# Dense weights and the experts' gate and up matrices stored in HBM in the blocks in which they are loaded

## The chip, the core and the metric

The kernel runs on one core of a Trainium2 chip. The metric is the device time of one execution in microseconds. Before the change it is 3160.01 us, the median of three runs (3159.78 to 3161.74).

The engines are named as in the profile: PE is TensorE (matmul; PEld its weight loads), DVE is VectorE, ACT is ScalarE, POOL is GpSimd and SP is SyncE, which here only issues loads. HBM is the memory outside the core; SBUF is the memory on it, with 128 partitions. An array is fetched from HBM into SBUF by a DMA, which 16 transfer engines carry out in packets; a packet is one contiguous run of bytes.

## The reference

Three layers work on 256 tokens of width 2048, all in float32. What matters here is which weights they read.

```python
u = x @ w_in                                # [256, 2048] @ [2048, 10544]
y_r = _rwkv7_mixer(u_r, ...)                # a recurrence over the tokens, 16 heads
y_m = _mlstm_mixer(u_m, ...)                # a gated linear attention, 8 heads
mix = (sigmoid(g_r) * (y_r @ w_br) + sigmoid(g_m) * (y_m @ w_bm)) @ w_out
x = _layer_norm(ALPHA * x + mix)
moe = _hier_moe(x, ...)                     # 32 experts, two per token:
#       (silu(xb @ w_gate[e]) * (xb @ w_up[e])) @ w_down[e]
ple = sigmoid(x @ w_pg) * (p @ w_ple)
x = _layer_norm(ALPHA * x + moe + ple)
# second block, even layer: rmsnorm, x @ w_in_even [2048, 6144],
#   banded attention and a state-space scan (S5) with w_glu, then @ w_out_even
# second block, odd layer: rmsnorm, x @ w_in_odd [2048, 8208],
#   causal attention with a forget gate, 16 heads of 128, then @ w_out_odd
```

An expert's `w_gate` and `w_up` are [2048, 512] and its `w_down` is [512, 2048], 4 MiB each.

## The kernel before

**Dense products.** The class `Stream` holds a list of pieces. A piece is a block of a weight matrix of 512 KB and the products that use it. `cols` (line 124) takes 4 row blocks of 128 rows by 256 columns and computes the transposed output, 24 matmuls of 256 columns a piece; `rows` (line 158) takes 2 row blocks by 512 columns, 12 matmuls of 512 columns a piece. Each weight is split into a high part and a low part: `split` (line 265) copies the raw piece `wraw` into `whi` on ScalarE (line 266) and subtracts on VectorE to get `wlo` (line 267; on GpSimd in a few places). Each product is then made three times (lines 147, 149, 151, or 173 to 175): high by high, high by low, low by high.

`step` (line 83) emits the products of one piece at a time. Before that it splits up to two pieces ahead and issues the fetches of two or three raw buffers more. `weave` (line 111) puts such steps between the steps of the dependent chains (recurrence, attention, S5, routing), so that the dense products fill TensorE while a chain waits. The fetch of a piece is one DMA on SP's queue:

```python
def load(self, src):                                              # line 121
    return lambda raw: self.nc.sync.dma_start(raw, src.rearrange("(k p) n -> p k n", p=128))
```

The source is a slice of the matrix as the reference has it, row by row. A partition of the destination gets one row out of each row block: in `cols` 4 runs of 256 floats (1 KB each), in `rows` 2 runs of 512 floats (2 KB each). The runs of neighbouring partitions lie one matrix row apart: 10544 floats in `w_in`, 6144 in `w_in_even`, 8208 in `w_in_odd`, 2048 in `w_out` and most others.

At the start `lora` (line 386) has a piece of 96 columns that are gathered from three places in `w_in`: for each of its four fetches VectorE clears a part of the raw buffer and SP issues three narrow loads (32, 8 and 8 columns).

**Experts.** `expert_order` (line 1219) lists the loads of all 32 experts in the order of use: gate and up by turns in four steps of 512 rows each, then down in four steps of 128 rows, 1 MiB each. `load_expert` (line 1244) takes the next one into a ring of ten buffers `ew` of [128, 2048] and issues it on SP; the first ten go on ScalarE's queue during the out projection, and two more go into a spare tile. A partition gets 4 runs of 2 KB of gate or up, or one run of 8 KB of down. Experts go in pairs: gather of the tokens (line 1273), gate and up (line 1320), the activation on ScalarE and VectorE (lines 1328 and 1329), transposes (line 1332), down (line 1376), and the weighted sum back to the tokens (line 1304). The products with `w_pg` and `w_ple` are woven into the first pairs.

`overflow` (line 1170) is a loop over the experts for tokens past 64 an expert; it runs only when there are any.

**Odd layer.** `odd` (line 1851) queues a 16-column piece, and then for each of eight groups of 256 columns the pieces of k, q and z (4 each, by `cols`), with 8 pieces of v (by `rows`) ahead of every second group, and weaves the attention of 16 heads among them, three steps of the stream to one of the chain. SP's queue also carries two small loads `nk<-cum` for each head.

**What sets the order.** The order in which each engine runs its instructions is written by a planner when the kernel is built (`schedule_with_timeline_sim=True`, line 2194), which has its own estimates of times; `issue_after` pins some instructions behind others. The arrays are laid out on the host before the launch (`prep`, line 2129).

Of the kernel before, what the change touches and what calls it, by code (L numbers as in the profile page):

```python
# [16 lines left out]
D = 2048  # L17
S = 256
KT = D // 128
KCH = 4  # L20
# [16 lines left out]
# column offsets of w_in  # L37
# [4 lines left out]
class Piece:  # L42
    """a block of a weight matrix and the products that use it, in steps"""
# [5 lines left out]
class Stream:  # L49
    """dense products, emitted step by step; the weights are fetched and split ahead of their use"""  # L50
    AHEAD = 2

    def __init__(self, K):
        self.K, self.nc = K, K.nc
        self.pieces, self.nf, self.ns, self.nm, self.sub = [], 0, 0, 0, 0
        # instructions of ScalarE and GpSimd that the splits come after, with the low parts on GpSimd
        self.after = None
# [25 lines left out]
    def step(self):  # L83
        """one step of products (about 1.3 us of TensorE); False when none is left"""
# [38 lines left out]

    def cols(self, w, r0, kts, c0, ncols, xh, xl, evac, cw=256, fetch=None):
        """out^T[cols, tok] = (x @ w[:, c0:c0+ncols])^T; evac(tile of 128 columns, psum [m, 256])"""
        nc, K = self.nc, self.K
        for c in range(0, ncols, cw):
# [3 lines left out]
            for k0 in range(0, kts, KCH):  # L131
# [3 lines left out]
                else:  # L135
                    f = self.load(w[r0 + k0 * 128:r0 + (k0 + kn) * 128, c0 + c:c0 + c + n])
# [46 lines left out]
    def tokens_first(self, n):  # L183
        """the last n pieces, of rows(): token tile 0 of all of them before token tile 1"""
# [11 lines left out]
class Sums:  # L196
    """2^(1/4) x1 and what is added to it [128, 2, D], in a tile that is taken at the first sum"""
# [4 lines left out]
    def __call__(self, i, q, src):  # L202
        """src added to columns 512 q .. of token tile i"""
# [12 lines left out]
class Ker:  # L216
# [60 lines left out]
    def recip1p(self, t):  # L277
        """1 / (1 + t) in place"""
# [4 lines left out]
    def shift(self, out, ps, mu, omu):  # L283
        """out [m, 256] from psum [m, 256]"""
# [4 lines left out]
    # ================= RWKV-7 =================  # L289
    def rwkv_consts(self, pool):  # L290
# [18 lines left out]
        # blocks of 16: minus row j of its block on each partition; the block's mask; unit rows; halves of 32  # L309
# [71 lines left out]
    def sig(self, t):  # L381
        """sigmoid in place"""
# [3 lines left out]
    def lora(self, pool, xh, xl, ig, fg):  # L386
        """zw | za | zg and the mLSTM's gate logits"""
# [13 lines left out]
        self.st.cols(A["w_in"], 0, KT, C_L, 256, xh, xl, evac)  # L401
# [20 lines left out]
        self.st.cols(None, 0, KT, 0, 96, xh, xl, evac2, fetch=fetch)  # L422
# [7 lines left out]
    def rwkv_proj(self, q, W, C, xh, xl):  # L430
        """k, r, v of heads 4q .. 4q + 3: two tiles of 128 channels each"""
        cx = {}
        for nm, mu, c, pool in (("k", "mu_k", C_K, W), ("r", "mu_r", C_R, W), ("v", "mu_v", C_V, C)):
# [8 lines left out]
            self.st.cols(self.A["w_in"], 0, KT, c + 256 * q, 256, xh, xl, evac)  # L442
# [28 lines left out]
    def rwkv_prep(self, q, W, C, cx):  # L471
        """the factors of the chunked form, before the chains"""
# [16 lines left out]
        # decay and in-context rate  # L489
# [15 lines left out]
        # L = cumsum of sigmoid in each chunk; the log decay is -KAPPA * L  # L505
# [21 lines left out]
        # kk = k * k_k, normalised over each head  # L527
# [24 lines left out]
        # k' = k * (1 + (a - 1) k_a)  # L552
# [13 lines left out]
        # bonus  # L566
# [14 lines left out]
    def rwkv_post(self, q, C, cx, y):  # L581
        """head norm (v was centred, so d is: its mean square is the variance), bonus, gate"""
# [52 lines left out]
    def rwkv_pair(self, i, W2, cx):  # L635
        """two heads: the delta rule in four chunks of 64 tokens"""
# [1561 lines left out]
```

## Time and profile before

| | before |
|---|---|
| median of 3 runs | 3160.01 us (3159.78 to 3161.74) |
| span of the profiled execution | 3162.0 us; of the time around it the page shows nothing |
| TensorE matmul busy | 2922.4 us, 92% |
| VectorE, ScalarE, GpSimd busy | 49%, 33%, 16% |
| read from HBM | 727.00 MB, 235 GB/s over the span |
| packets | 441588; 229904 of them under 2 KB, 424592 under 8 KB |
| dense loads of 512 KB | 560 (`w_in` 164, `w_in_odd` 128, `w_in_even` 96, four matrices with 32, two with 16, `w_glu` 8, `w_ple` 4) |
| expert loads of 1 MiB | 384 |

The page's slices show the stages: the first layer's mixers from 0 to about 950 us, the experts to about 2050, the even layer to about 2530, the odd layer to about 3115, then the final norm. Busy time of TensorE is modelled to the end of each matmul's pipeline, so consecutive matmuls overlap in it, and a matmul at the lower of the two clocks (1.2 instead of 2.4 GHz) is busy longer. "PEclk" is the mean granted share of the full clock in a stretch. The DMA share is the mean busy share of the 16 transfer engines; in a full queue it comes out a little above 1.

### The profile page before, as it was taken

The page shows a single profiled execution, that of the slowest core. Times are in us where ns is not written, and L with a number is a line of the kernel's source. Part 1 is how long each engine was busy: PE and PEld are TensorE (multiplying, and loading weights), DVE is VectorE, ACT ScalarE, POOL GpSimd, SP SyncE. Part 2 cuts the span into 40 slices and gives each one's busy share as a digit, 9 for nine tenths or more (in the row PEclk, how much of TensorE's full clock was granted, in tenths as well). Part 3 has the DMA queues.
Part 4 walks back from the last instruction along what each step waited for, and adds up shares of the span by engine and source line. Part 5 has one row for each costly group of instructions (what it writes and reads, how often), then busy time and mean ns, then how long its engine had stood idle before and what let it go on. Part 6 is the DMA issues. An engine that isn't in the chain of part 4 may idle for free.

```text
span 3162.0 us, 48985 instructions
## 1 busy us (share of the span) xinstructions
PE 2922.4 (92%) x20107; PEld 2311.8 (73%) x20107; DVE 1535.3 (49%) x2382; ACT 1054.6 (33%) x1741; POOL 520.8 (16%) x554
## 2 busy tenths in 40 slices
PE   8999999889989999999899999789899999889978
PEld 8988888889876666565555545478688879779867
DVE  6776855885462212221121112388986654334334
ACT  4433434554332111111010000245554444334333
POOL 4121111760010000000000000165653000000000
PEclk9999999999999999999999999999999999989989
DMA  6433343876769999999999999755555658887874
GB/s 179 135 97 84 96 134 107 242 217 196 272 242 339 348 393 383 376 362 372 363 395 399 395 399 395 281 179 171 167 164 158 201 144 163 139 136 160 147 128 167
DMA packets 441588, 744.95 MB, mean 236 GB/s; under 512 B 28928, under 2 KB 229904, under 8 KB 424592
## 3 DMA queue, kind: packets, MB, share of 16 engines
q1 hardware_dynamic: 430480, 716.60, 71.3%
q10 hardware_dynamic: 9984, 22.02, 2.0%
q0 software_dynamic: 896, 3.15, 0.4%
q8 instruction: 160, 2.62, 0.3%
q14 instruction: 68, 0.56, 0.1%
HBM read 727.00 MB, written 14.70 MB: 235 GB/s over the span
## 4 chain that ended last, share of the span: by engine, by line
PE 52%; DMA 15%; DVE 14%; issue 13%; POOL 3%; ACT 3%; SPq 0%; ACTq 0%; DVEq 0%; POOLq 0%
PE acc L1320 10%; DMA wraw<-in_w_in_odd 8%; PE acc L151 6%; PE mx L1376 6%; PE acc L147 5%; PE acc L149 5%; DVE wlo L267 5%; PE mx L1304 3%; PE mx L1273 3%; PE acc L174 2%; PE acc L173 2%; PE acc L175 2%; ACT whi L266 2%; DMA ew<-in_w_up 2%; DMA wraw<-in_w_out 2%
## 5 line engine op out<-in xcount | busy, mean ns | idle before, releaser
L267 DVE TENSOR_TENSOR wlo<-wraw,whi 128x1024 fp32r<-128x1024 f32 x563 | 718.0, 1277 | 652.9 <-ACT whi L266 649.3
L266 ACT CAST whi<-wraw 128x1024 fp32r<-128x1024 f32 (+1 forms) x568 | 588.3, 1038 | 842.7 <-PE acc L149 276.3
L147 PE MATMUL acc<-xh,whi 128*128 128x256 f32 (+1 forms) x2624 | 761.4, 291 | 64.1 <-ACT whi L266 52.3
L151 PE MATMUL acc<-xh,wlo 128*128 128x256 f32 (+1 forms) x2624 | 762.9, 292 | 56.7 <-DVE wlo L267 56.3
L149 PE MATMUL acc<-xl,whi 128*128 128x256 f32 (+1 forms) x2624 | 754.5, 288 | 1.7 <-DVE xl L267 1.7
L147 PEld LDWEIGHTS acc<-xh,whi 128*128 128x128 f32 (+1 forms) x2624 | 510.4, 195 | 81.0 <-ACT whi L266 58.8
L151 PEld LDWEIGHTS acc<-xh,wlo 128*128 128x128 f32 (+1 forms) x2624 | 509.8, 195 | 76.8 <-DVE wlo L267 71.1
L149 PEld LDWEIGHTS acc<-xl,whi 128*128 128x128 f32 (+1 forms) x2624 | 511.4, 195 | 8.9 <-issue 4.3
L1320 PE MATMUL acc<-ew,xg 128*64 128x256 f32 x4096 | 463.1, 382 | 13.6 <-DMA ew<-in_w_down 5.3
L1320 PEld LDWEIGHTS acc<-ew,xg 128*64 128x64 f32 x4096 | 297.0, 137 | 171.6 <-issue 22.6
L1376 PE MATMUL mx<-ew,eht 128*64 128x512 f32 x976 | 224.2, 602 | 11.7 <-DVE eht L1334 10.6
L1329 DVE TENSOR_TENSOR eh<-eh,acc 128x256 f32<-128x256 f32 x32 | 13.5, 421 | 447.4 <-ACT eh L1328 447.4
L1295 POOL TENSOR_TENSOR ero<-oh,wt 128x128 f32<-128x128 f32 x32 | 12.9, 402 | 1068.2 <-PE mx L1296 1060.1
L1376 PEld LDWEIGHTS mx<-ew,eht 128*64 128x64 f32 x976 | 67.4, 137 | 132.8 <-issue 106.8
L174 PE MATMUL acc<-wlo,xh 128*128 128x512 f32 x384 | 153.8, 400 | 5.1 <-DVE wlo L267 5.0
L175 PE MATMUL acc<-whi,xl 128*128 128x512 f32 x384 | 151.8, 395 | 0.0
L173 PE MATMUL acc<-whi,xh 128*128 128x512 f32 x384 | 144.6, 402 | 0.0
L1275 ACT COPY xg<-mx 128x512 f32<-128x512 f32 x64 | 37.5, 585 | 311.1 <-PE mx L1273 311.1
L1382 DVE COPY ey<-mx 64x512 f32<-64x512 f32 x62 | 43.0, 694 | 201.8 <-ACT ey L1384 201.7
L1273 PEld LDWEIGHTS mx<-oh,z 128*128 128x128 f32 x1024 | 118.4, 192 | 13.2 <-issue 12.9
L1273 PE MATMUL mx<-oh,z 128*128 128x128 f32 x1024 | 121.6, 277 | 0.0
L1304 PE MATMUL mx<-ey,er 128*128 128x512 f32 x248 | 110.9, 599 | 4.6 <-ACT er L1298 3.9
(606 smaller groups left out, 3965.2 us busy)
## 6 DMA issues: line engine op xcount, KB each, us to landing
ew<-in_w_gate SPq DMA_DIRECT2D x124, 1024.0 KB, 14.1
ew<-in_w_up SPq DMA_DIRECT2D x124, 1024.0 KB, 14.1
ew<-in_w_down SPq DMA_DIRECT2D x124, 1024.0 KB, 13.8
wraw<-in_w_in SPq DMA_DIRECT2D x164, 512.0 KB, 3.7
wraw<-in_w_in_odd SPq DMA_DIRECT2D x128, 512.0 KB, 7.3
wraw<-in_w_in_even SPq DMA_DIRECT2D x96, 512.0 KB, 4.2
wraw<-in_w_out SPq DMA_DIRECT2D x32, 512.0 KB, 6.6
wraw<-in_w_pg SPq DMA_DIRECT2D x32, 512.0 KB, 9.4
```

The lines of the kernel that those rows point to most:

```text
L147: nc.tensor.matmul(ps, p.hi[:, k, m], xh[:, kk], start=kk == 0 and i == 0, stop=False, skip_group_check=True)
L149: nc.tensor.matmul(ps, p.hi[:, k, m], xl[:, kk], start=False, stop=False, skip_group_check=True)
L151: nc.tensor.matmul(ps, p.lo[:, k, m], xh[:, kk], start=False, stop=last, skip_group_check=True)
L173: nc.tensor.matmul(acc[i], xh[:, kk, m], p.hi[:, k], start=kk == 0, stop=False)
L174: nc.tensor.matmul(acc[i], xh[:, kk, m], p.lo[:, k], start=False, stop=False)
L175: mm = nc.tensor.matmul(acc[i], xl[:, kk, m], p.hi[:, k], start=False, stop=last)
L266: self.last_split = self.nc.scalar.copy(hi, src).ins
L267: (eng or self.nc.vector).tensor_sub(lo, src, hi.bitcast(F32))
L1273: m = nc.tensor.matmul(ps[:, 128 * k:128 * k + 128], x1[:, i, kk:kk + 128], oh[:, i].rearrange("p e s -> p (e s)"), start=i == 0, stop=i = ...
L1304: nc.tensor.matmul(po, r[:, i], y[:, q], start=True, stop=True)
L1320: nc.tensor.matmul(ps[64 * g:64 * g + 64], xg[:, k0 + k, j], w[:, k, 256 * g:256 * g + 256], start=w is wg and k0 + k == 0, stop=k0 + k == ...
L1376: nc.tensor.matmul(py[b][64 * g:64 * g + 64, :], ht[:, k % 2, k // 2], wd[:, 0, c:c + 512], start=k == 0, stop=k == 3, tile_position=(0, 6 ...
```

## The change

The host stores the dense matrices, and the experts' gate and up, as blocks: each block is one fetch, and within a block all bytes of a partition are contiguous. A dense piece becomes 4 KB a partition, a block of gate or up 8 KB a partition. `w_in`, `w_in_even` and `w_in_odd` are cut by use into several arrays (`w_rkv`, `w_qk`, `w_lif`, `w_mv`, `w_o`, `w_g`; `we_qk`, `we_v`, `we_u`; `wo_qkz`, `wo_v`, `wo_f`). The 96 gathered columns of `lora` become an array of their own, with zeros in the gaps, so that the clearing and the three narrow loads of each fetch become one load (1536 bytes a partition). The 16-column piece of the odd layer has 256 bytes a partition instead of 4 runs of 64. `w_down`, the small matrices and the loads of activations stay. In `overflow` the slices of the new arrays keep runs of 1 KB. Comments are dropped as well.

```diff
     def load(self, src):
-        return lambda raw: self.nc.sync.dma_start(raw, src.rearrange("(k p) n -> p k n", p=128))
+        return lambda raw: self.nc.sync.dma_start(raw.rearrange("p k n -> p (k n)"), src)
...
-    def cols(self, w, r0, kts, c0, ncols, xh, xl, evac, cw=256, fetch=None):
+    def cols(self, w, kts, c0, ncols, xh, xl, evac, cw=256, fetch=None):
...
-                    f = self.load(w[r0 + k0 * 128:r0 + (k0 + kn) * 128, c0 + c:c0 + c + n])
+                    f = self.load(w[(c0 + c) // cw, k0 // KCH])
...
-    def rows(self, w, r0, kts, c0, ncols, xh, xl, evac):
+    def rows(self, w, kp0, kts, c0, ncols, xh, xl, evac, load=None):
...
-                p = Piece(self.load(w[r0 + k0 * 128:r0 + (k0 + 2) * 128, c0 + c:c0 + c + 512]), 2, 512)
+                f = load(c0 + c, kp0 + k0 // 2) if load else self.load(w[(c0 + c) // 512, kp0 + k0 // 2])
+                p = Piece(f, 2, 512)
...
-        def fetch(k0, kn):
-            rows = slice(k0 * 128, (k0 + kn) * 128)
-
-            def f(raw):
-                nc.vector.memset(raw[:, :, 32:96], 0.0)
-                for d, c, n in ((0, C_L + 256, 32), (32, C_IF, 8), (64, C_IF + 8, 8)):
-                    nc.sync.dma_start(raw[:, :, d:d + n],
-                                      A["w_in"][rows, c:c + n].rearrange("(k p) n -> p k n", p=128))
-            return f
...
-        self.st.cols(None, 0, KT, 0, 96, xh, xl, evac2, fetch=fetch)
+        self.st.cols(A["w_lif"], KT, 0, 96, xh, xl, evac2)
...
     def expert_order(self):
...
-                rows = slice(128 * k0, 128 * k0 + 512)
-                yield A["w_gate"][e, rows]
-                yield A["w_up"][e, rows]
+                yield A["w_gate"][e, k0 // 4]
+                yield A["w_up"][e, k0 // 4]
...
     def load_expert(self, eng=None, t=None):
...
-        v = t.rearrange("p (k n) -> p k n", n=src.shape[1])
-        (eng or self.nc.sync).dma_start(v, src.rearrange("(k p) n -> p k n", p=128))
+        v = t.rearrange("p (k n) -> p k n", n=src.shape[2])
+        if src.shape[1] == 4:
+            (eng or self.nc.sync).dma_start(t, src.rearrange("p k n -> p (k n)"))
+        else:
+            (eng or self.nc.sync).dma_start(v, src)
...
-            for nm, c0 in (("k", 2048), ("q", 0), ("z", 6144)):
+            for nm, c0 in (("k", 2048), ("q", 0), ("z", 4096)):
...
-                st.cols(w, 0, KT, c0 + 256 * c, 256, xh, xl, f)
+                st.cols(A["wo_qkz"], KT, c0 + 256 * c, 256, xh, xl, f)
...
+def _blocks(w, cw, kn):
+    k, n = w.shape
+    v = w.reshape(k // (128 * kn), kn, 128, n // cw, cw).transpose(3, 0, 2, 1, 4)
+    return np.ascontiguousarray(v).reshape(n // cw, k // (128 * kn), 128, kn * cw)
+
+def _by_cols(w, cw=256):
+    return _blocks(w, cw, KCH)
+
+def _by_rows(w):
+    return _blocks(w, 512, 2)
...
+    for n in ("w_gate", "w_up"):
+        a[n] = f(n)[0].reshape(32, 4, 4, 128, 512).transpose(0, 1, 3, 2, 4)
```

## Rows read from the trace of the kernel before

**Rows 1.** Page: the span, and TensorE's busy time.

```profile
span 3162.0 us, 48985 instructions
...
PE 2922.4 (92%) x20107; PEld 2311.8 (73%) x20107; DVE 1535.3 (49%) x2382; ACT 1054.6 (33%) x1741; POOL 520.8 (16%) x554
```

**Rows 2.** Page: the chain that ended last, shares by line.

```profile
PE acc L1320 10%; DMA wraw<-in_w_in_odd 8%; PE acc L151 6%; PE mx L1376 6%; PE acc L147 5%; PE acc L149 5%; DVE wlo L267 5%; PE mx L1304 3%; PE mx L1273 3%; PE acc L174 2%; PE acc L173 2%; PE acc L175 2%; ACT whi L266 2%; DMA ew<-in_w_up 2%; DMA wraw<-in_w_out 2%
```

**Rows 3.** Page: issues of loads; count, size, median us to landing.

```profile
wraw<-in_w_in SPq DMA_DIRECT2D x164, 512.0 KB, 3.7
wraw<-in_w_in_odd SPq DMA_DIRECT2D x128, 512.0 KB, 7.3
```

**Rows 4.** Windows: us, busy per engine (count), granted clock, DMA share, GB/s.

```profile
2740.00:2825.00 85.00, 64.36 (x393) 58.65 (x392) 26.80 (x36) 25.49 (x46) 2.06 (x3) 0.84 0.83 111
2825.00:2985.00 160.00, 153.52 (x1063) 143.36 (x1062) 72.64 (x89) 70.74 (x112) 4.47 (x6) 0.98 0.81 165
...
2060.00:2450.00 390.00, 349.39 (x2510) 306.85 (x2509) 333.38 (x436) 197.52 (x387) 218.64 (x195) 0.99 0.55 168
```

**Rows 5.** Tile `wraw`, 2744 to 2813 us: splits, ns min/median/max, first and last start.

```profile
L266 ACT CAST whi<-wraw x11: 1044/1045/1047, 2746.2 to 2808.1; 128x1024 fp32r<-128x1024 f32 x11
```

**Rows 6.** Waits of TensorE, 2595 to 3115 us: total, times, longest.

```profile
PE acc L147 <- ACT whi L266: 36.1, 25, 2.8
PE acc L151 <- DVE wlo L267: 16.3, 24, 0.9
PE acc L147 <- ACT oq L1889: 2.9, 3, 1.3
...
PE acc L173 <- DVE res L1842: 0.5, 1, 0.5
```

**Rows 7.** Lines, TensorE, 2595 to 3115 us: count | busy us, mean ns | idle before.

```profile
L147 PE MATMUL acc<-xh,whi 128*128 128x256 f32 x768 | 229.9, 300 | 42.0 <-ACT whi L266 36.1 <-ACT oq L1889 2.9 <-ACT ok L1889 2.8
...
L174 PE MATMUL acc<-wlo,xh 128*128 128x512 f32 x100 | 40.1, 401 | 0.1
...
L174 PE MATMUL acc<-wlo,oh 128*128 128x512 f32 x72 | 28.6, 397 | 0.0
...
L1910 PE MATMUL mx<-ok,oq 128*128 128x256 f32 x32 | 10.4, 410 | 0.0
...
L1627 PE MATMUL mx<-ident,ae 128*128 128x128 f32 x16 | 4.5, 281 | 0.0
```

**Rows 8.** Timeline of TensorE, two fed runs in the odd layer: start, us.

```profile
2841.62 0.39 PE L174 MATMUL acc<-wlo,xh 128*128 128x512 f32 x1
...
2843.43 0.39 PE L174 MATMUL acc<-wlo,xh 128*128 128x512 f32 x1
...
2901.80 0.28 PE L147 MATMUL acc<-xh,whi 128*128 128x256 f32 x1
...
2903.84 0.28 PE L151 MATMUL acc<-xh,wlo 128*128 128x256 f32 x1
```

**Rows 9.** DMA view, packets by size: 984 to 990 us, then 1685 to 1692.

```profile
DMA packets 347, 2.53 MB, mean 422 GB/s; under 512 B 38, under 2 KB 38, under 8 KB 38
...
DMA packets 1354, 2.70 MB, mean 386 GB/s; under 512 B 43, under 2 KB 43, under 8 KB 1353
```

**Rows 10.** Windows as above, over one pair and over five pairs of experts.

```profile
1585.87:1646.98 61.11, 58.20 (x408) 33.46 (x407) 10.36 (x19) 5.79 (x11) 0.80 (x2) 1.00 1.03 397
1646.98:1965.33 318.35, 294.66 (x2032) 165.50 (x2031) 51.37 (x89) 28.95 (x55) 3.98 (x10) 1.00 1.03 397
```

**Rows 11.** Waits of TensorE, 1646.98 to 1965.33 us.

```profile
PE mx L1332 <- DVE eh L1329: 9.4, 10, 0.9
PE acc L1320 <- DMA ew<-in_w_up: 5.2, 7, 1.3
```

**Rows 12.** Waits of TensorE, 800 to 960 us.

```profile
PE acc L174 <- DVE wlo L267: 2.8, 5, 0.8
```

**Rows 13.** Waits of TensorE, 2060 to 2450 us.

```profile
PE acc L151 <- DVE wlo L267: 24.8, 17, 3.4
```

More of the change, by code (lines that the diff above doesn't have):

```diff
@@ L441, in evac @@
                     cx[nm] = cx["part_" + nm]
-            self.st.cols(self.A["w_in"], 0, KT, c + 256 * q, 256, xh, xl, evac)
+            self.st.cols(self.A["w_rkv"], KT, c + 256 * q, 256, xh, xl, evac)
         return cx
@@ L813, in evac_qk @@
             cx["n"] += 1
-        self.st.cols(A["w_in"], 0, KT, C_QK, 1024, xh, xl, evac_qk)
+        self.st.cols(A["w_qk"], KT, 0, 1024, xh, xl, evac_qk)
         V = W.tile([128, 2, 1024], F32, name="mv")
@@ L826, in evac_v @@
             cx["n"] += 1
-        self.st.rows(A["w_in"], 0, KT, C_MV, 1024, xh, xl, evac_v)
+        self.st.rows(A["w_mv"], 0, KT, 0, 1024, xh, xl, evac_v)
         cx["qk"], cx["V"], cx["pool"] = qk, V, W
@@ L838, in evac_o @@
             cx["n"] += 1
-        self.st.cols(self.A["w_in"], 0, KT, C_O, 1024, xh, xl, evac_o)
+        self.st.cols(self.A["w_o"], KT, 0, 1024, xh, xl, evac_o)
         cx["so"] = so
@@ L957, in ev @@
                     nc.scalar.activation(g[nm, i], ps, AF.Tanh, scale=0.5, bias=hb[:, b + i:b + i + 1])
-                st.cols(A["w_in"], 0, KT, C_G + 128 * off + 256 * c, 256, xh, xl, ev)
+                st.cols(A["w_g"], KT, 128 * off + 256 * c, 256, xh, xl, ev)
         def br(c):
@@ L964, in ev @@
                 nc.vector.scalar_tensor_tensor(g["r", i], g["r", i], 1.0, ps, op0=OP.add, op1=OP.mult)
-            st.cols(A["w_br"], 0, 8, 256 * c, 256, yrh, yrl, ev)
+            st.cols(A["w_br"], 8, 256 * c, 256, yrh, yrl, ev)
         def bm(c):
@@ L973, in ev @@
                 self.split_half(mh[:, 2 * c + i], ml[:, 2 * c + i], g["r", i])
-            st.cols(A["w_bm"], 0, 8, 256 * c, 256, ymh, yml, ev)
+            st.cols(A["w_bm"], 8, 256 * c, 256, ymh, yml, ev)
         for c in range(0, 8, 2):
@@ L1194, in overflow @@
             with tc.For_i(0, 32, 1) as e:
-                row = lambda n: A[n][bass.ds(e, 1)].rearrange("o r c -> (o r) c")
+                gu = lambda n, c: lambda k0, kn: lambda raw: nc.sync.dma_start(
+                    raw, A[n][bass.ds(e, 1), k0 // KCH, :, :, c:c + 256].rearrange("o p k n -> (o p) k n"))
+                dn = lambda c, kp: lambda raw: nc.sync.dma_start(
+                    raw, A["w_down"][bass.ds(e, 1), 256 * kp:256 * kp + 256, c:c + 512].rearrange(
+                        "o (k p) n -> (o p) k n", p=128))
                 wc = new("w", (128, 2))
@@ L1211, in ev_d @@
                         nc.vector.scalar_tensor_tensor(v, ps, wc[:, i:i + 1], v, op0=OP.mult, op1=OP.add)
-                    st.cols(row("w_gate"), 0, KT, c, 256, xh, xl, ev_g)
-                    st.cols(row("w_up"), 0, KT, c, 256, xh, xl, ev_u)
+                    st.cols(None, KT, 0, 256, xh, xl, ev_g, fetch=gu("w_gate", c))
+                    st.cols(None, KT, 0, 256, xh, xl, ev_u, fetch=gu("w_up", c))
                     st.run()
-                    st.rows(row("w_down"), c, 2, 0, D, hh, hl, ev_d)
+                    st.rows(None, c // 256, 2, 0, D, hh, hl, ev_d, load=dn)
                     st.run()
@@ L1635, in even @@
         nc, A, st = self.nc, self.A, self.st
-        w = A["w_in_even"]
         u = W.tile([128, 8, S], F32, name="u")
@@ L1653, in f @@
                 done.add(("u", T))
-            st.cols(w, 0, KT, 3072 + 256 * c, 256, xh, xl, f)
+            st.cols(A["we_u"], KT, 256 * c, 256, xh, xl, f)
         def ev_v(c):
@@ L1661, in f @@
                 done.add(("v", c, i))
-            st.rows(w, 0, KT, 2048 + 512 * c, 512, xh, xl, f)
+            st.rows(A["we_v"], 0, KT, 512 * c, 512, xh, xl, f)
         def ev_kq(c):
@@ L1670, in f @@
                     done.add(("kq", c, j, i))
-                st.cols(w, 0, KT, c0 + 256 * c, 256, xh, xl, f)
+                st.cols(A["we_qk"], KT, c0 + 256 * c, 256, xh, xl, f)
         def ev_za(c):
@@ L1679, in f @@
                 done.add(("za", c, i))
-            st.cols(w, 0, KT, 4096 + 256 * c, 256, xh, xl, f)
+            st.cols(A["we_u"], KT, 1024 + 256 * c, 256, xh, xl, f)
         def attention():
@@ L1777, in ev_glu @@
                     self.split_half(yh[:, k], yl[:, k], szb[:, k])
-        st.cols(A["w_glu"], 0, 8, 0, 1024, yh, yl, ev_glu)
+        st.cols(A["w_glu"], 8, 0, 1024, yh, yl, ev_glu)
         res(0, 2, 4)
@@ L1926, in attention @@
                 self.split_half(oh[:, h], ol[:, h], o)
-        st.cols(w, 0, KT, 8192, 16, xh, xl, ev_f)
+        st.cols(A["wo_f"], KT, 0, 16, xh, xl, ev_f)
         for c in range(8):
@@ L2160, in prep @@
     a["pk"] = pk
-    for n in ("w_in", "w_w2", "w_a2", "w_g2", "w_br", "w_bm", "w_out", "w_gate", "w_up", "w_down", "w_pg", "w_ple"):
+    for n in ("w_w2", "w_a2", "w_g2", "w_down"):
         a[n] = f(n)[0]
-    for n in ("w_in_even", "w_glu", "w_out_even", "w_in_odd", "w_out_odd"):
-        a[n] = f(n + "_2")[0]
+    w = f("w_in")[0]
+    a["w_rkv"], a["w_qk"] = _by_cols(w[:, :C_L + 256]), _by_cols(w[:, C_QK:C_MV])
+    lif = np.zeros((D, 96), np.float32)
+    lif[:, :32], lif[:, 32:40], lif[:, 64:72] = w[:, C_L + 256:C_QK], w[:, C_IF:C_IF + 8], w[:, C_IF + 8:C_O]
+    a["w_lif"] = _by_cols(lif, 96)
+    a["w_mv"], a["w_o"], a["w_g"] = _by_rows(w[:, C_MV:C_IF]), _by_cols(w[:, C_O:C_G]), _by_cols(w[:, C_G:])
+    for n in ("w_br", "w_bm"):
+        a[n] = _by_cols(f(n)[0])
+    for n in ("w_out", "w_pg", "w_ple"):
+        a[n] = _by_rows(f(n)[0])
+    for n in ("w_gate", "w_up"):
+        a[n] = f(n)[0].reshape(32, 4, 4, 128, 512).transpose(0, 1, 3, 2, 4)
+    w = f("w_in_even_2")[0]
+    a["we_qk"], a["we_v"], a["we_u"] = _by_cols(w[:, :2048]), _by_rows(w[:, 2048:3072]), _by_cols(w[:, 3072:])
+    w = f("w_in_odd_2")[0]
+    a["wo_qkz"] = np.concatenate([_by_cols(w[:, :4096]), _by_cols(w[:, 6144:8192])])
+    a["wo_v"], a["wo_f"] = _by_rows(w[:, 4096:6144]), _by_cols(w[:, 8192:], 16)
+    a["w_glu"] = _by_cols(f("w_glu_2")[0])
+    for n in ("w_out_even", "w_out_odd"):
+        a[n] = _by_rows(f(n + "_2")[0])
     idx = np.clip(128 + np.arange(128)[:, None] - np.arange(256)[None, :], -128, 128) + 128
```

14 lines of the change are left out of this document (6 added, 8 removed).

## The prediction

> **What bounds the kernel now.** I read the page from the top: TensorE is busy 2922.4 of 3162.0 us, 92% [rows 1]. That leaves at most about 240 us of plain idle time, so a faster transfer is worth something only where TensorE runs dry behind it. The chain that ended last says where to look: loads of `in_w_in_odd` hold 8% of it (about 250 us), and `ew<-in_w_up` and `wraw<-in_w_out` 2% each; no other load is among its largest shares [rows 2]. The issue table shows why the first stands out: the same 512 KB take 7.3 us to land from `in_w_in_odd` and 3.7 us from `in_w_in` [rows 3]. So three stretches are read closely: the odd layer, the experts, and the rest of the dense stages.
>
> In the odd layer the reader is to see transfer engines that are 0.81 to 0.83 busy and yet move only 111 to 165 GB/s [rows 4]. At a full share that is 111 / 0.83 = 134 GB/s in the worst stretch and 165 / 0.81 = 204 in the better one. In the worst one ScalarE's splits follow each other every 6.19 us (10 gaps in 61.9 us) [rows 5], and TensorE, starved, was granted a mean clock of 0.84 [rows 4], so part of its time ran at 1.2 instead of 2.4 GHz and counts as busy.
>
> **The change, part by part.** No matmul, split or evacuation is added or removed by the new layout, and there are as many large loads as before. What changes is how the source of each load lies: 512-KB dense pieces go from rows of 1 KB (`cols`) or 2 KB (`rows`) a partition to 4 KB, gate and up from 2 KB to 8 KB; `w_down` stays.
>
> *Odd layer (2595 to 3115 us of the trace, 520 us).* What does TensorE need if no load is late? It issues 3 x 768 products of 256 columns and 299 + 218 = 517 of 512 columns there ([rows 7], where one of the three rows of each triple stands). In a fed run 17 steps of the first kind take 2.04 us, 0.120 us each, and 8 of the second 1.81 us, 0.226 us each [rows 8]. So 2304 x 0.120 = 276.5 and 517 x 0.226 = 116.8. The attention's products are seven rows from 10.4 down to 4.5 us busy, 46.4 together [rows 7]; a busy time overlaps its neighbours (0.300 us busy against 0.120 us apart), so they cost between 0.4 x 46.4 = 19 and 46; I take 26, near the overlapped end, since they too are issued back to back. The floor is 419 us. Waits on other things remain: four rows from 2.9 to 0.5, 8.2 us in all [rows 6]. 520 - 427 = **93 us** saved. Both ends: at most 520 - 412 = 108 (attention at its low end, no other wait); at least the idle that is visible behind the two splits, 36.1 + 16.3 = 52.4 [rows 6]. The difference between 52 and 93 is the half-rate clock, and gaps that the modelled ends of the matmuls hide.
>
> Will 4-KB rows feed it? A piece of 524,288 bytes per 24 x 0.120 = 2.88 us is 182 GB/s. No row shows weights in 4-KB rows; the neighbours are 2-KB rows, 386 GB/s (1310 of 1354 packets), and 8-KB rows, 422 GB/s (309 of 347 packets), both with a full queue [rows 9]. Either is twice the need, so the size matters little and what counts is that the slow address pattern goes. The matrix has 8208 columns, so neighbouring rows lie 32,832 bytes apart, 64 more than 32 KiB, and, counted by the issues, the loads crawl at the fourth and again at the eighth group of 256 columns: they follow addresses and not time. What is late next is TensorE itself: ScalarE and VectorE are busy 71 to 73 of 160 us there [rows 4].
>
> The Trainium skill (DMA: Bandwidth & Descriptors, Latency and other measured facts) says that row pitches at large powers of two halve the rate, that padding by 192 bytes does not cure it, and that tiles should be laid out contiguously. Its pitches start at 512 KiB, so it does not cover 32 KiB; the trace agrees in kind, 134 GB/s against 386 [rows 4, 9].
>
> *Experts.* From 1585.87 to 1646.98 a pair of experts took 61.1 us; the next five took 318.35, 63.7 each, at a transfer share of 1.03 [rows 10]; the bounds are starts of a pair's combine, line 1304. A pair loads 24 blocks of 1 MiB, 25.17 MB. While 2-KB packets of gate and up alone are under way the rate is 386 GB/s, while 8-KB packets of `w_down` are 422 [rows 9]; 16.78 MB at the one and 8.39 MB at the other is 63.3 us, about the pair time seen. All at 422 it is 59.6, below the 61.1 at which TensorE's own work, with its waits on VectorE (9.4 us at `eh` over five pairs), holds the pair [rows 11]. So the loads stop being last by a small margin and a pair takes 61.1: 5 x 2.6 = 13 us. The waits on loads that go include 5.2 us at `in_w_up` [rows 11]. The pairs before 1500 us have the dense pieces woven in and no such wait; 2 us for them. **15 us**; ends 0 (nothing gained per byte) and 30 (all pairs gain as these).
>
> *Other dense stages.* In the out projection the largest wait of TensorE behind a split is 2.8 us [rows 12]; I take 4 for all of them, ends 0 and 10. In the even layer TensorE waits 24.8 us for `wlo` [rows 13], but VectorE is busy 333 of 390 us there [rows 4], so most of it is VectorE's queue; I take 4, ends 0 and 25. In the first three stages and at the start, 5, ends 0 and 10: four fetches of three narrow loads and a VectorE memset each become four single loads, which takes eight issues out of SP's queue ahead of the dense loads and four memsets out of VectorE's, all at the start only.
>
> Sum: 93 + 15 + 4 + 4 + 5 = 121 us off the span of 3162.0. The runs' median is 3160.0, 2 us from that span, so I subtract from the median: **3039 us**.
>
> The order of each engine's instructions comes from a planner with its own estimate of a load's time. Whether it changes cannot be read from the trace; I allow 15 us to either side.
>
> **The rivals.**
> *The experts gain nothing (3054).* The plateau of 386 GB/s could be the memory's and not the rows'. Then 15 us fall away. Against it: `w_down` passes 386 by 9% in the same queue [rows 9].
> The Trainium skill (DMA: Bandwidth & Descriptors, Specifications) gives an HBM limit of about 358 GB/s a core, by which longer rows could not help the experts. The measured 422 is above it, so that rule gets a low chance.
>
> *The odd layer gives only its visible idle (3080).* If the hidden part is not clock and gaps but the products' own pace, 52 replaces 93: 3160 - 80. For it: a busy TensorE stands in most slices. Against it: in the stretches of 160 and 85 us the counts are 1063 and 393 products, 6.6 and 4.6 a us, at the same mixture roughly [rows 4].
>
> *More comes free (3000).* Odd layer 108, all pairs 30, even and the rest 22: 160 us. It needs VectorE's waits in the even layer to be loads in disguise.
>
> *The blocks collide: slower.* Contiguous pieces put neighbouring partitions 4096 bytes apart, a power of two. If that met the same slow path as the odd matrix, 134 GB/s, each of the 560 dense pieces would take 3.91 us instead of 2.88, and the kernel 560 x 1.03 - 121 = 456 us more, 3616. It decides at the rate where 560 x (time - 2.88) eats the 121 us: 3.10 us a piece, 169 GB/s. Against it: `w_down`'s blocks are contiguous with 8192 bytes a partition, as regular a pattern, and run at 422 [rows 9].
>
> *The change does not do what it says (3160).* The loads could still be cut into 1- or 2-KB packets. Against it: `w_down`'s 8-KB rows do move as 8-KB packets [rows 9].
>
> **How the numbers follow.** Forecast 0.60, its own range 3015 to 3062; experts gain nothing 0.12; visible idle only 0.12; more comes free 0.08; blocks collide 0.04; no effect 0.04. The range 3005 to 3090 holds the first three nearly whole, so about 0.82, with the planner's 15 us inside it. What a measurement of this kernel can tell from no change is about 0.2%, 6 us; all cases but the last two lie far beyond it, so faster 0.92, same 0.04, slower 0.04.
>
> **What would show it.** Odd layer: landing of its dense loads near 4 us instead of 7.3, granted clock 0.97 or more throughout, and the stretch at 425 us; if it stays above 460, the step from idle to clock was wrong. Packets: under 2 KB almost gone from the count. Experts: pairs after 1500 us at 61 us, waits at `ew` near nothing, and a rate of about 410 GB/s; if pairs stay at 63.7 the first rival holds. Even layer: `wlo` waits above 15 us confirm VectorE's queue. The prediction is wrong as a whole if any contiguous stage moves its pieces at under 182 GB/s with a full queue.

## The result, and the profile after

The kernel after takes 3049.82 us (median of 4 runs, 3043.89 to 3053.66), the kernel before in the same runs 3160.88 (4 runs). The ratio is 0.9643, 95% interval 0.9626 to 0.9661: 111 us faster. The forecast was 3039, its range 3005 to 3090. The profiled execution took 3049.12 us, of which the span is 3047.3; the spans of the two traces differ by 114.7 us, and the terms below are compared with that.

The page of the kernel after, its span, TensorE, the chain by line and the packets, answers to [rows 1, 2]:

```profile
span 3047.3 us, 48960 instructions
...
PE 2881.9 (95%) x20107; PEld 2295.4 (75%) x20107; DVE 1535.2 (50%) x2378; ACT 1056.8 (35%) x1741; POOL 521.2 (17%) x554
...
DMA packets 171124, 745.35 MB, mean 245 GB/s; under 512 B 21120, under 2 KB 36240, under 8 KB 121360
...
PE 33%; DVE 7%; issue 5%; POOL 2%; DMA 1%; ACT 1%; SPq 0%; DVEq 0%; POOLq 0%; ACTq 0%
PE acc L1320 7%; PE acc L153 4%; PE acc L151 4%; PE acc L149 4%; PE mx L1376 4%; DVE wlo L271 2%; PE mx L1273 2%; PE mx L1304 2%; PE acc L177 2%; PE acc L178 2%; PE acc L179 2%; DVE s5a L1802 1%; POOL s5a L1807 1%; DVE tw L1806 1%; POOL s5a L1798 0%
```

The chain as the page follows it now covers only half of the span (its shares add up to 49%): it reaches back to 1528 us, into the experts. In that part all loads together hold 1%; none of gate or up is in it, and the loads of the odd matrix, 8% before, are not among its lines here. Of `in_w_out`, whose loads end before 920 us, it says nothing. Packets under 2 KB went from 229904 to 36240. In the kernel after, the two splits are lines 270 and 271, the products of `cols` 149, 151 and 153, those of `rows` 177 to 179; lines 1320, 1332, 1376, 1304 and 1599 are the same in both.

Stages are cut at the first combine of the experts (line 1304) and at the two groups of line 1599, the norm ahead of the even and of the odd layer. The times are starts of those instructions in the traces:

| stage | before, us | after, us | difference | forecast |
|---|---|---|---|---|
| start to the first product of the out projection | 821.4 | 823.1 | +1.8 | -5 |
| out projection (first to last product with `w_out`) | 96.5 | 90.9 | -5.5 | -4 |
| from there to the first combine | 96.4 | 95.9 | -0.6 | |
| first combine to the even layer | 1039.4 | 1025.8 | -13.6 | -15 |
| even layer | 507.6 | 507.1 | -0.5 | -4 |
| odd layer and final norm | 600.7 | 504.4 | -96.3 | -93 |

*Odd layer.* The windows of the kernel after, over the stretch in which the end of the third group of columns, the whole fourth and the pieces of v behind it are loaded (it answers to [rows 4]), over the fed middle of the layer, and over the whole of it (columns: us, busy per engine with counts, granted clock, DMA share, GB/s):

```profile
2690.00:2775.00 85.00, 85.00 (x615) 80.73 (x614) 44.01 (x56) 42.54 (x71) 3.41 (x4) 1.00 0.57 179
2580.00:3000.00 420.00, 418.57 (x2986) 395.20 (x2985) 208.70 (x255) 206.64 (x333) 11.56 (x15) 1.00 0.57 182
2542.88:3047.26 504.38, 493.05 (x3360) 457.62 (x3360) 254.47 (x315) 241.64 (x383) 16.88 (x21) 0.99 0.55 177
```

The kernel before, in the same columns, over the 520 us from which the prediction took its count of products, and over its whole odd layer:

```profile
2595.00:3115.00 520.00, 458.72 (x2997) 420.10 (x2996) 207.18 (x255) 204.82 (x333) 12.80 (x16) 0.94 0.79 148
2561.32:3162.00 600.68, 529.36 (x3360) 479.14 (x3360) 253.15 (x315) 239.82 (x383) 17.73 (x21) 0.94 0.75 148
```

In 85 us TensorE now makes 615 products where it made 393 [rows 4]. The transfer engines are busy 0.57 of the time and move 179 GB/s, 314 at a full share, where they moved 111 at 0.83. Over the layer the same 3360 matmuls leave 600.68 - 529.36 = 71.3 us idle before and 504.38 - 493.05 = 11.3 after: 60 us of the gain are idle time, the other 36 are busy time, with a granted clock of 0.99 in place of 0.94. The prediction's stretch held 2997 products in 520 us; now 2986 take 420, where 427 was forecast.

Tile `wraw` of the kernel after, 2690 to 2760 us (ns min/median/max, first and last start), answers to [rows 5]:

```profile
L270 ACT CAST whi<-wraw x23: 1032/1047/1053, 2692.8 to 2758.1; 128x1024 fp32r<-128x1024 f32 x23
```

The splits follow each other every 65.3 / 22 = 2.97 us, where it was 6.19. The landing of the loads on the page (count, KB, median us) answers to [rows 3]:

```profile
ew<-in_w_gate SPq DMA_DIRECT2D x124, 1024.0 KB, 9.4
ew<-in_w_up SPq DMA_DIRECT2D x124, 1024.0 KB, 10.0
...
wraw<-in_wo_qkz SPq DMA_DIRECT2D x96, 512.0 KB, 4.2
...
wraw<-in_wo_v SPq DMA_DIRECT2D x32, 512.0 KB, 3.6
```

All of TensorE's waits in the kernel after from 2580 to 3000 us, which answer to [rows 6]:

```profile
PE acc L153 <- DVE wlo L271: 0.8, 1, 0.8
PE acc L177 <- DVE res L1841: 0.5, 1, 0.5
```

*Experts.* Windows of the kernel after over one pair and the five pairs behind it, which answer to [rows 10]:

```profile
1580.69:1641.80 61.11, 58.20 (x408) 33.46 (x407) 10.37 (x19) 5.80 (x11) 0.80 (x2) 1.00 1.01 415
1641.80:1947.36 305.56, 291.00 (x2033) 167.31 (x2031) 51.34 (x89) 28.98 (x55) 4.00 (x10) 1.00 1.01 413
```

And TensorE's waits from 1641.8 to 1947.36 us, which answer to [rows 11]:

```profile
PE mx L1332 <- DVE eh L1329: 9.4, 10, 0.9
PE mx L1376 <- DVE eht L1334: 5.2, 10, 0.5
```

The five pairs take 61.1 us each instead of 63.7. The waits on VectorE stay, 9.4 us at `eh` as before; the 5.2 us at `in_w_up` are gone. The 291.0 us in which TensorE is busy and the two waits of 9.4 and 5.2 us fill the 305.6, so TensorE sets this pace now. The 25.17 MB of a pair in 61.1 us are 412 GB/s: the 413 in the window is what this pace asks for, so it need not be the most that the loads can do, though a share of 1.01 leaves little room.

*Even layer and out projection.* TensorE's longest wait behind a split in the kernel after, from 2042 to 2432 us, the same place in the even layer as [rows 13]:

```profile
PE acc L153 <- DVE wlo L271: 23.6, 16, 3.4
```

The one from 800 to 960 us, which answers to [rows 12]:

```profile
PE acc L178 <- DVE wlo L271: 1.7, 3, 0.8
```

### The profile page after: what moved, and what is told of

Its sections match the earlier page's. It is cut to its first block, busy times and chain, and to the rows that moved or that the text cites. A ratio compares the mean times of both kernels' runs of the same rounds, so it can differ in the third digit from the quotient of the medians.

```text
span 3047.3 us, 48960 instructions
## 1 busy us (share of the span) xinstructions
PE 2881.9 (95%) x20107; PEld 2295.4 (75%) x20107; DVE 1535.2 (50%) x2378; ACT 1056.8 (35%) x1741; POOL 521.2 (17%) x554
## 5 line engine op out<-in xcount | busy, mean ns | idle before, releaser
L153 PE MATMUL acc<-xh,wlo 128*128 128x256 f32 (+1 forms) x2624 | 752.2, 288 | 40.8 <-DVE wlo L271 40.8
L149 PE MATMUL acc<-xh,whi 128*128 128x256 f32 (+1 forms) x2624 | 750.8, 287 | 20.2 <-ACT whi L270 13.7
L153 PEld LDWEIGHTS acc<-xh,wlo 128*128 128x128 f32 (+1 forms) x2624 | 502.9, 192 | 54.1 <-DVE wlo L271 48.5
L149 PEld LDWEIGHTS acc<-xh,whi 128*128 128x128 f32 (+1 forms) x2624 | 503.0, 192 | 30.0 <-ACT whi L270 14.6
L151 PEld LDWEIGHTS acc<-xl,whi 128*128 128x128 f32 (+1 forms) x2624 | 504.0, 192 | 8.3 <-issue 4.3
```

Of the source, the lines that this page charges most:

```text
L149: nc.tensor.matmul(ps, p.hi[:, k, m], xh[:, kk], start=kk == 0 and i == 0, stop=False, skip_group_check=True)
L151: nc.tensor.matmul(ps, p.hi[:, k, m], xl[:, kk], start=False, stop=False, skip_group_check=True)
L153: nc.tensor.matmul(ps, p.lo[:, k, m], xh[:, kk], start=False, stop=last, skip_group_check=True)
```

## The experiments

The theory after the result: the odd layer's 96 us come from the addresses of the strided loads of `w_in_odd`, not from the size of their packets; the experts' 13 us come from the longer runs of gate and up; the other edits are worth a few us. TensorE's, ScalarE's and GpSimd's instructions stand in the same order in both kernels, but for two neighbouring products of the even layer's attention, so the planner is left out of it. What the order could not say is which property of the addresses hurts.

"Odd layer" below is measured as in the table. The kernel before took 3162.57 us in the runs of the first four, 3170.44 with the next three, 3165.4 with the last four.

**e1, the odd matrix alone.** The kernel before with `w_in_odd` alone in blocks:

```diff
-            st.rows(w, 0, KT, 4096 + 512 * c, 512, xh, xl, f)
+            st.rows(A["wo_v"], 0, KT, 512 * c, 512, xh, xl, f)
...
-                st.cols(w, 0, KT, c0 + 256 * c, 256, xh, xl, f)
+                st.cols(A["wo_qkz"], 0, KT, c0 + 256 * c, 256, xh, xl, f)
```

> The kernel before, with only the odd layer's matrix w_in_odd in blocks (4 KB a partition); experts and all other dense pieces as before. Theory (the odd layer's loads were late because of where their rows lie): the odd layer, from its first transposed product (line 1599, second group) to the end, shrinks from 600.7 us to about 505, as in the kernel after; the whole to 3064, ratio 0.970. Rival (the stages help each other, for instance through the clock): less than 80 us of the 96 come from this edit alone, ratio above 0.975.

Measured: 3062.6 us, ratio 0.9683 (0.9657 to 0.971); odd layer 502.0 us. The whole odd term belongs to this edit.

**e2, dense blocks, short runs.** As e1, but a block holds its row blocks one behind the other: 512 KB without gaps, in runs of 1 KB (2 KB for v), so as many packets as before.

```diff
-        return lambda raw: self.nc.sync.dma_start(raw.rearrange("p k n -> p (k n)"), w[j, k])
+        return lambda raw: self.nc.sync.dma_start(raw, w[j, k].rearrange("k p n -> p k n"))
```

> As e1_odd_only, but inside each contiguous 512-KB block the runs stay as they were: 1 KB a partition and row block (2 KB for v), 128 partitions side by side. So the addresses are dense and the packets are as small as before. Theory (addresses): all of the gain of e1, within 5 us: ratio 0.970. Rival (packet size: the 1-KB packets themselves were too slow): no gain, ratio 1.00; loads of the odd layer still land after 7 us.

Measured: 3068.1 us, ratio 0.9703 (0.9676 to 0.973); odd layer 502.0, packets 441588 as in the kernel before. Addresses, not the length of the runs.

**e3, the old layout with rows 4 KB longer.** 36,928 bytes between rows instead of 32,832; the same strided runs.

```diff
+    a["w_in_odd"] = np.pad(a["w_in_odd"], ((0, 0), (0, 1024)))
```

> The kernel before, with 1024 columns of padding behind w_in_odd, so that a row is 36,928 bytes instead of 32,832; the same loads of 1- and 2-KB runs, nothing contiguous. Theory in its narrow form (the pitch close to 32 KiB is what hurts): most of the gain of e1, 80 us or more, ratio 0.975 or less. Rival (any strided pattern of 1-KB runs over so large a matrix is slow here): no gain, ratio 1.00.

Measured: 3064.6 us, ratio 0.9686 (0.9659 to 0.9714); odd layer 502.2. The window over the odd layer of this kernel, and then its loads on the page:

```profile
2561.50:3063.70 502.20, 491.17 (x3360) 456.03 (x3360) 254.28 (x315) 241.67 (x383) 18.52 (x21) 0.99 0.56 178
```

```profile
wraw<-in_w_in_odd SPq DMA_DIRECT2D x128, 512.0 KB, 3.6
```

A strided load is as good as a contiguous one here, if the rows lie another distance apart. So contiguity is a sufficient cure and not a necessary one.

**e4, exactly 32 KiB.** The 16 columns of f in an array of their own; 8192 columns are left, 32,768 bytes a row.

```diff
+    a["w_odd_f"], a["w_in_odd"] = a["w_in_odd"][:, 8192:], a["w_in_odd"][:, :8192]
```

> The kernel before, with the 16 columns of the forget gate in a matrix of their own, so that a row of w_in_odd is exactly 32,768 bytes. Theory (closeness to 32 KiB hurts): as slow as before or slower, ratio 1.00 to 1.03. Rival (the 64 bytes over 32 KiB hurt, since they put the rows off 256-byte boundaries): faster, ratio 0.97 to 0.98.

Measured: 3065.1 us, ratio 0.9694 (0.9665 to 0.9723); odd layer 501.3. The window over its odd layer, and its loads:

```profile
2560.96:3062.30 501.34, 490.86 (x3360) 455.98 (x3360) 253.72 (x315) 241.67 (x383) 20.27 (x21) 1.00 0.57 178
```

```profile
wraw<-in_w_in_odd SPq DMA_DIRECT2D x128, 512.0 KB, 3.8
```

A miss: I held closeness to a power of two to be the cause, and the power of two itself is fast. That rows begin 64 bytes off a multiple of 256 is not the cause by itself either, since e3's 36,928 bytes leave the same remainder and are fast.

**e5, gate and up alone** in blocks of 8 KB a partition:

```diff
-                yield A["w_gate"][e, rows]
-                yield A["w_up"][e, rows]
+                yield A["w_gate"][e, k0 // 4]
+                yield A["w_up"][e, k0 // 4]
```

> The kernel before, with only the experts' gate and up in blocks (8 KB a partition). Theory (2-KB packets held the later pairs of experts at 63.7 us): pairs after 1500 us at 61.1 us, the stage from its first combine to the even layer 13 us shorter; ratio 0.9957. Rival (another part of the change, as the dense pieces of w_pg, freed the experts): no change, ratio 1.00.

Measured: 3151.6 us, ratio 0.9944 (0.9922 to 0.9965). From the first combine to the even layer 1026.3 us, the kernel after's time within 0.5 us, and the late five pairs:

```profile
1652.25:1957.82 305.57, 291.01 (x2033) 167.38 (x2031) 51.37 (x89) 28.95 (x55) 3.98 (x10) 1.00 1.01 413
```

The experts' term comes from this edit alone. (The profiled execution, 3163.2 us, is one of the longest of this kernel: its out projection starts at 829.6 us and its odd layer takes 605.8, neither of which the edit touches. So traces are compared by stages here, and not by their sum.)

**e6, everything but these two.** The kernel after with `w_in_odd` as before, and gate and up in runs of 2 KB:

```diff
-                yield A["w_gate"][e, k0 // 4]
-                yield A["w_up"][e, k0 // 4]
+                yield A["w_gate"][e, k0 // 4].rearrange("k p n -> p k n")
+                yield A["w_up"][e, k0 // 4].rearrange("k p n -> p k n")
...
-                st.cols(A["wo_qkz"], KT, c0 + 256 * c, 256, xh, xl, f)
+                st.cols(A["w_in_odd"], KT, c0 + 256 * c, 256, xh, xl, f)
```

> The kernel after, with the odd layer's w_in_odd and the experts' gate and up as before; all other dense matrices in blocks (w_out_odd and w_lif too). From the traces of before and after: the stretch up to the first combine 4.4 us shorter, the even layer 0.5: 4 to 6 us in all, ratio 0.9985. The prediction had 13 us for these stages, ratio 0.996.

Measured: 3102.7 us, ratio 0.9785 (0.976 to 0.9811), far more than expected. First combine at 1012.6 us and even layer 508.8, little moved as expected. The surprise is the odd layer: 541.7 us instead of 600.7, though its array and its loads are those of before. The windows of this kernel over the late five pairs and over the odd layer, and the landing of its odd loads:

```profile
1649.00:1967.00 318.00, 295.25 (x2032) 165.80 (x2031) 51.55 (x89) 28.96 (x55) 3.99 (x10) 1.00 1.03 397
2558.38:3100.10 541.72, 507.13 (x3360) 463.14 (x3360) 253.61 (x315) 240.58 (x383) 18.05 (x21) 0.99 0.66 165
```

```profile
wraw<-in_w_in_odd SPq DMA_DIRECT2D x128, 512.0 KB, 5.9
```

TensorE's, ScalarE's and GpSimd's instructions stand in the order of the kernel before. What differs for this layer is the other arrays, which have other sizes and names, so the odd matrix may lie at another place in HBM. That how badly it crawls depends on the place is an inference: no trace shows where an array lies. The first window is the rest of e5's answer: a block of gate or up is 1 MiB without gaps in both layouts, and with 2-KB runs the rate stays at 397 GB/s. There it is the length of the runs that counts.

**e7, the groups in another order.** The kernel before with its column groups in the order 3, 4, 1, 2, 7, 8, 5, 6, and the heads of the attention likewise:

```diff
-            for h in range(16):
+            for h in (4, 5, 6, 7, 0, 1, 2, 3, 12, 13, 14, 15, 8, 9, 10, 11):
...
-        for c in range(8):
+        for c in (2, 3, 0, 1, 6, 7, 4, 5):
```

> The kernel before, with the odd layer's column groups in the order 2, 3, 0, 1, 6, 7, 4, 5 (heads accordingly). Theory (addresses): the loads that crawl, 6 us a piece, move from the fourth and eighth place in time to the second and sixth. Rival (time: something that happens in those places, such as the loads of nk): they stay at the fourth and eighth place. The total stays within 15 us.

First the windows of the kernel before while its third, fourth, seventh and eighth group are loaded:

```profile
2720.00:2734.00 14.00, 13.51 (x111) 13.46 (x112) 6.19 (x7) 5.09 (x8) 0.00 (x0) 1.00 0.84 159
2772.00:2801.00 29.00, 20.61 (x116) 19.08 (x115) 6.79 (x10) 6.89 (x13) 0.73 (x1) 0.74 0.91 92
2961.60:2978.00 16.40, 14.85 (x112) 14.44 (x113) 6.88 (x7) 6.47 (x9) 0.00 (x0) 0.94 0.83 151
3014.00:3041.00 27.00, 20.23 (x118) 18.61 (x119) 6.42 (x10) 6.41 (x12) 0.00 (x0) 0.76 0.91 93
```

Measured: 3165.8 us in one run, odd layer 597.9. The windows of this kernel while its second, fourth, sixth and eighth group in time are loaded:

```profile
2657.00:2703.00 46.00, 31.23 (x196) 28.19 (x197) 11.82 (x16) 10.15 (x17) 0.73 (x1) 0.85 0.84 93
2783.00:2810.00 27.00, 25.68 (x198) 24.34 (x199) 11.24 (x15) 10.67 (x19) 1.47 (x2) 1.00 0.91 169
2893.00:2940.00 47.00, 33.19 (x191) 30.41 (x191) 11.35 (x16) 10.63 (x18) 0.74 (x1) 0.76 0.87 90
3020.00:3049.00 29.00, 26.25 (x210) 25.41 (x210) 12.02 (x15) 11.89 (x21) 1.48 (x2) 1.00 0.91 165
```

The crawl (90 to 93 GB/s) has moved to the second and sixth place in time, where the fourth and the eighth group of columns now stand. It follows the addresses, as the prediction read from the issues.

**e8, the same matrix 1 KB further up.**

```diff
-        w = A["w_in_odd"]
+        w = A["w_in_odd"][256:256 + 2048 * 8208].rearrange("(r c) -> r c", c=8208)
...
+    a["w_in_odd"] = np.pad(a["w_in_odd"].ravel(), (256, 0))
```

> The kernel before, with the same matrix of pitch 32,832 bytes moved up by 1 KB in HBM (256 floats in front of it); loads, order and packets are unchanged. Before, the loads crawled (about 6 us a piece) at the fourth and eighth groups of 256 columns, which start 3 KB past a multiple of 4 KB from the array's first byte. Theory: how a load goes is set by its absolute address within 4 KB. Then what crawled at the fourth and eighth groups crawls one group earlier, at the third and seventh, and the odd layer stays near 600 us. Rival: a matrix at another place behaves differently as a whole, as when the other arrays changed around it (541.7 us); then the crawl stays in its groups and the layer lands anywhere between 505 and 600. Third: it is set by the place within the array alone; then the crawl stays at the fourth and eighth and the layer at 600 +- 3.

Measured: 3159.4 us in one run, odd layer 596.9. The windows of this kernel while its third, fourth, seventh and eighth group are loaded, in the order of before:

```profile
2709.00:2757.00 48.00, 32.55 (x177) 29.55 (x178) 10.32 (x13) 10.83 (x18) 0.73 (x1) 0.73 0.85 89
2777.00:2806.00 29.00, 25.52 (x198) 25.21 (x197) 11.28 (x16) 10.52 (x18) 0.74 (x1) 0.94 0.65 151
2953.50:3000.00 46.50, 32.05 (x172) 28.93 (x173) 9.33 (x9) 8.37 (x11) 0.00 (x0) 0.72 0.86 86
3020.00:3046.00 26.00, 25.11 (x204) 24.59 (x204) 13.34 (x17) 11.70 (x20) 1.48 (x2) 1.00 0.75 178
```

With 1 KB in front, the crawl moves from the fourth and eighth group to the third and seventh, which now begin 3 KB past a multiple of 4 KB from the array's first byte. That is what the theory of the address within 4 KB said, and neither rival did. But what is shown is only which start of a group is slow: each further row begins 64 bytes further on, 8 KB over the 128 rows of a row block, so the rows of every group pass through all places within 4 KB, and why one start is worse than another is not shown.

**e9 and e10, the neighbouring distances.** Rows padded by 16 columns (32,896 bytes apart) and by 48 (33,024):

```diff
+    a["w_in_odd"] = np.pad(a["w_in_odd"], ((0, 0), (0, 16)))     # e10: 48
```

> The kernel before with the odd matrix's rows padded by 16 columns: 32,896 bytes apart, 128 more than 32 KiB instead of 64. Theory: the crawl belongs to the one pitch of 32,832 and its place; then the odd layer takes about 502 us as with the pitches of 32,768 and 36,928. Rival: every pitch a little over 32 KiB drifts slowly through the same places of the memory and crawls; then the layer takes over 550 us and landing is 6 us or more.

> The same with 48 columns more: 33,024 bytes apart, 256 more than 32 KiB. Theory of the one pitch: about 502 us for the odd layer. Rival (slow drift): the drift is four times as fast as before, so slower than 510 us yet under 600. If 32,896 crawls and this does not, the bound of the drift lies between.

Measured, one run each: 3069.3 and 3065.7 us, odd layer 502.3 and 502.5. The loads of e9, then of e10:

```profile
wraw<-in_w_in_odd SPq DMA_DIRECT2D x128, 512.0 KB, 4.0
```

```profile
wraw<-in_w_in_odd SPq DMA_DIRECT2D x128, 512.0 KB, 4.3
```

64 bytes more a row cure all of it; a slow drift past 32 KiB is not what hurts. Padding also makes the array larger, so it may move it; where it lies no trace shows.

**e11, the kernel after with the odd matrix undone.**

```diff
-                st.cols(A["wo_qkz"], KT, c0 + 256 * c, 256, xh, xl, f)
+                st.cols(A["w_in_odd"], KT, c0 + 256 * c, 256, xh, xl, f)
```

> The kernel after, with the odd matrix alone stored and loaded as before (pitch 32,832, 1- and 2-KB runs). If the terms add up, its ratio to before is 1 - 18.5/3162 = 0.994 when the odd layer crawls as before (600 us). But where the array lies in HBM has changed with the other arrays; if the severity depends on that, as in the run with gate and up undone as well (541.7 us), the odd layer takes between 505 and 600 and the ratio falls accordingly: 541.7 would give 0.975. The stages before the odd one should stand as in the kernel after: first combine at about 1010 us and 1026 from there to the even layer.

Measured: 3091.5 us, ratio 0.976 (0.9738 to 0.9781); first combine at 1009.2, 1026.1 us from there to the even layer, which takes 512.3, and the odd layer 541.6. The odd layer is e6's to 0.1 us, in another program with arrays of the same sizes, so the severity is no accident of a run. The windows of this kernel while its third, fourth, seventh and eighth group are loaded:

```profile
2695.00:2719.00 24.00, 24.00 (x199) 23.84 (x198) 11.21 (x14) 12.25 (x21) 0.73 (x1) 1.00 0.62 176
2734.00:2765.00 31.00, 25.95 (x191) 24.60 (x192) 11.32 (x16) 11.07 (x19) 1.44 (x2) 0.95 1.03 139
2906.00:2930.00 24.00, 24.00 (x197) 23.79 (x196) 10.40 (x11) 10.70 (x14) 0.00 (x0) 1.00 0.58 173
2946.00:2976.00 30.00, 26.29 (x196) 24.92 (x197) 11.73 (x17) 11.60 (x20) 1.47 (x2) 0.96 1.04 148
```

The same two groups crawl, at 139 and 148 GB/s instead of 92 and 93. So which groups crawl stayed with the layout of the matrix, and how badly changed with the other arrays.

## Why the prediction was right

**Odd layer, 93 forecast, 96.3 measured.** The step from visible idle (52.4) to the whole (93) was the one in doubt, and it held: the waits behind the two splits went from 52.4 to 0.8 us, and 96.3 - 51.6 = 45 us came beside them, against the 41 that the floor of counted products gave. The stretch of that floor, forecast at 427 us, took 420. The rival of the visible idle alone would have left the layer at about 548. "The size matters little" is shown by e2. The 4-KB blocks do not collide: 314 GB/s at a full share, far above the 169 at which that rival decided. Other distances between the rows do as well as blocks (e3, e4, e9, e10).

The cause the prediction left at "64 more than 32 KiB". My own first reading of that, nearness to a power of two, fell with e4. What is shown: of the five distances tried, 32,768, 32,896, 33,024 and 36,928 bytes give 501 to 503 us, and only 32,832 crawls (e3, e4, e9, e10); at that distance the column groups that crawl move with a shift of 1 KB (e8); and the same matrix in a program with other arrays takes 541.7 (e6, e11). The four that do well also changed the array's size, and so perhaps its place; against that as the cause, six programs at 32,832 (before, e5 to e8, e11) take 542 to 606 us with the array at whatever places they gave it, and none comes near 503. Why 32,832 is bad, and what about the other arrays made 542 of 600, the traces do not show: no view has the memory's own addresses. It stays open.

The Trainium skill (DMA: Bandwidth & Descriptors, Latency and other measured facts) advises a few KiB more of pitch, or contiguous tiles, and says that 192 bytes did not help at a pitch of 4 MiB. Both of its cures hold here. The rest does not carry over to these short pitches: 192 bytes more (e10) cured as fully as 4 KiB (e3), and a power of two fed the layer as well (e4).

**Experts, 15 forecast, 13.6 measured.** The late pairs gave 318.35 - 305.56 = 12.8 us for the 13 of the sum, and stopped at the 61.1 us that was read as TensorE's own pace. The ten kernels with the old layout of gate and up take 1035.5 to 1039.4 us from the first combine to the even layer, the three with the new one (after, e5, e11) 1025.8 to 1026.3: the term is 9 to 14 us, and 13.6 is its upper end. The rate came out at 413 GB/s, between the 386 and 422 of [rows 9]. The 2 us for the early pairs did not come: their eight pairs took 571.5 us before and 570.7 after, within the 568.8 to 571.5 of kernels that leave them unchanged. The rival "nothing gained per byte" is refuted by e5 against the kernel before: 413 and 397 GB/s, and nothing but the layout of gate and up, the length of its runs, between the two kernels (e6, the kernel after with the short runs and the old odd matrix put back, has 397 again). The limit of 358 GB/s that the Trainium skill gives (DMA: Bandwidth & Descriptors, Specifications) did not bind on this one core.

**Out projection, 4 forecast, 5.5 measured.** The size was right, the place only in part: behind `wlo` 2.8 us became 1.7 [rows 12]. The stretch is 90.9 us where both the dense pieces and gate and up are in blocks (after, e11), 94.4 with gate and up alone (e5), 93.9 with the dense pieces alone (e6), and 93.9 to 96.7 in the eight that leave it as it was (e1 to e4, e7 to e10). The two edits' own shares can't be told apart at that scatter; the first ten expert loads run in this stretch too.

**Even layer, 4 forecast, 0.5 measured.** The term was mis-sized; the layer takes 507.0 to 509.4 us in the nine experiments that leave it alone and 508.8 and 512.3 in the two with blocks (e6, e11), so even the 0.5 is not told from nothing. `wlo` waits 23.6 us where it waited 24.8 [rows 13], above the 15 that the prediction named for VectorE's queue: that reading was right, and should have given the value 0 or 1.

**Start and first stages, 5 forecast, none measured** (+1.8 by the trace). The out projection starts between 820.5 and 829.6 us in the nine experiments with the old start, and between 822.5 and 823.1 in the three kernels with the new one (after, e6, e11). If the eight issues and four memsets cost anything, it is less than this scatter; the prediction should have put them at 0.

Together: 121 forecast, 114.7 measured by the spans; of the difference 6.8 is the first stages, 3.5 the even layer and 1.4 the experts, less 3.3 that the odd layer and 2.1 that the out projection and what follows it gave on top. The medians moved by 111, so the forecast is 11 us low: 6 by the terms, the rest by the scatter of executions around their median. That scatter is larger than the 0.2% of the prediction: in the 14 runs beside e5 to e7 the kernel before took 3156.9 to 3180.9 us. The 111 us lie far beyond it.

## What to carry to other kernels

When a load's engines are busy and its bytes are few, look at the distance between its rows before its packet size: here 64 bytes of padding a row took the stage from 600.7 to 502.3 us (e9), as much as blocks did (502.0, e1). Look for it by address: if the slow pieces come again at a fixed step of columns and move with the order of the loads, it is the pattern. Longer runs paid where the transfer queue was full all the time, as with the experts (e5); where it had slack, in the odd layer, they were worth nothing (e2).

## What the runs showed of the hardware

- Loads of 128 x 4 runs of 1 KB whose rows lie 32,832 bytes apart moved at 86 to 93 GB/s at their worst (e7, e8); with 32,768, 32,896, 33,024 or 36,928 between the rows the layer ran at TensorE's pace.
- With that distance the slow groups of columns were the two whose first row begins 3 KB past a multiple of 4 KB, counted from the array's first byte (each further row begins 64 bytes further on); 1 KB in front moved them by one group (e8). With other arrays around it the same two groups were slow at 139 and 148 GB/s (e11). In the worst stretches the granted clock fell as well, 0.72 to 0.73 against 0.94 to 1.00 in the others (e8): TensorE was starved there, and its time at the lower of the two clocks is part of the price.
- The other groups were slowed too, without starving TensorE as much: 159 GB/s at a share of 0.84 and 151 at 0.83 for the third and the seventh, 189 and 182 at a full share, where the layer with 36,928 bytes between the rows has 178 at 0.56, 318 at a full share (before, e3). The fed stretch of the kernel after takes 182.
- Expert blocks of 1 MiB without gaps went from 397 to 413 GB/s when a partition's share went from four runs of 2 KB to one of 8 KB, and landed after 9.4 to 10.0 us instead of 14.2 (e6 against the kernel after). At 413 TensorE waited for no load; stretches of 8-KB packets alone ran at 422 [rows 9].
